# Row-wise logsumexp: VectorE sums each row as two halves in one pass, and the loads are cut anew

## The chip, the cores and the metric

The kernel runs on one core of a Trainium2 chip. Its time is the device time of one execution in microseconds (us); four runs of the kernel before gave a median of 163.52, from 163.41 to 163.89. Beside these times there is a profile of one execution. The engines that matter here are ScalarE (ACT), VectorE (DVE) and SyncE (SP), whose queue issues the loads, and the 16 DMA engines that carry them. GpSimd (POOL) only sets four constants and TensorE (PE) does nothing.

## The reference

The input is 32 x 512 rows of 1024 float32 values, 67.1 MB; the output is one number a row:

```python
def reference(x, axis):                      # x: (32, 512, 1024), axis = -1
    x_max = np.max(x, axis=axis, keepdims=True)
    return (x_max.squeeze(axis)
            + np.log(np.sum(np.exp(x - x_max), axis=axis))).astype(np.float32)
```

Both kernels leave the maximum out: they compute log(sum(exp(x))), which is the same number for values of this size, drawn from a normal distribution.

## The kernel before

**Tiling.** The 16384 rows are spread over 128 partitions, 128 rows for each partition. "A row" below means one row in every partition at once, so there are 128 of them, each 4 KB in a partition and 512 KB in all. They are loaded in 17 pieces, called load 0 to load 16; the list `CHUNKS` gives, for each load, its rows and how many of these are summed by DVE.

**The ring.** Loaded rows lie in `ring`, which has room for 51 rows. Loads take consecutive slots; a load that does not fit before the end of the ring begins again at slot 0. SP issues the loads in order (L84). Before a load into slots that were used, SP waits until the rows that lay there have been finished, by a count of finished instructions of DVE (`dve_done`) and one of ACT (`act_done`). Since the queue is in order, a load that waits holds back those behind it.

**The work on a load.** ACT waits until the load has landed. It takes the exponential of the first `n_dve` rows in one instruction, in place (L115), and DVE then sums them, all rows of the load in one reduction (L120):

```python
            nc.vector.wait_ge(act_done, acts)
            nc.vector.reduce_sum(
                out=sums[:, row : row + n_dve], in_=ring[:, s : s + n_dve], axis=AX
            ).then_inc(dve_done, 1)
```

Each other row of the load gets an ACT instruction of its own (L127), which takes the exponential and also gives the sum; in the trace this is a pair, ACTIVATE and ACTIVATION_READ_ACCUMULATOR. The sums of all rows gather in `sums`.

**The logarithms.** `take_logs` (L92) takes Ln of a stretch of `sums` into `res`. It is called twice: early, when ACT comes to load `LN_AT`, for the rows of all loads before it, and at the end for the rest. It runs on ACT and waits for the DVE and ACT work on its rows. At last ACT's queue stores `res`, 64 KB, to the output.

**Order.** The program is written out by hand; each engine runs its instructions in the order of the loop over `CHUNKS`, and no scheduler moves anything.

Of the kernel before, what the change touches and what calls it, by code (L numbers as in the profile page):

```python
# [1 line left out]

# [4 lines left out]

CHUNKS = [  # L10
    (4, 1), (15, 11), (16, 10), (16, 15), (16, 0), (14, 0), (12, 9), (9, 5), (7, 5), (5, 4),
    (4, 3), (3, 0), (2, 2), (2, 2), (1, 0), (1, 0), (1, 0),
]
RING_ROWS = 51

LN_AT = 5


@with_exitstack
def kernel(  # L20
    ctx: ExitStack,
    tc: tile.TileContext,
    x: bass.AP,
    axis: bass.AP,
    out: bass.AP,
):
    nc = tc.nc
    P = nc.NUM_PARTITIONS

    assert axis in (-1, len(x.shape) - 1), f"only last-axis reduction supported, got {axis}"  # L30

    x_flat = x.flatten_outer_dims()
    N, D = x_flat.shape
    assert N % P == 0
    NB = N // P
    assert sum(r for r, _ in CHUNKS) == NB

    fp32 = mybir.dt.float32
    Exp = mybir.ActivationFunctionType.Exp
    Ln = mybir.ActivationFunctionType.Ln  # L40
    AX = mybir.AxisListType.X

    x_v = x_flat.rearrange("(p t) d -> p t d", p=P)
    out_v = bass.AP(tensor=out.tensor, offset=out.offset, ap=[[NB, P], [1, NB]])

    ring = nc.alloc_sbuf_tensor("ring", [P, RING_ROWS, D], fp32).ap()
    sums = nc.alloc_sbuf_tensor("sums", [P, NB], fp32).ap()
    res = nc.alloc_sbuf_tensor("res", [P, NB], fp32).ap()

    landed = [nc.alloc_semaphore(f"landed{i}") for i in range(len(CHUNKS))]  # L50
    act_done = nc.alloc_semaphore("act_done")
    dve_done = nc.alloc_semaphore("dve_done")
    stored = nc.alloc_semaphore("stored")
    used = sorted(sem.num for sem in [*landed, act_done, dve_done])
    assert used == list(range(used[0], used[0] + len(used)))


    hook = nc.pop_inst_callback()
    symbolic, nc._always_lower_symbolic_ap = nc._always_lower_symbolic_ap, False


    place = []
    row = slot = 0
    for r, _ in CHUNKS:
        if slot + r > RING_ROWS:
            slot = 0
        place.append((slot, row))
        slot += r
        row += r

    busy = [(0, 0)] * RING_ROWS
    acts = dves = 0

    def load(i):
        (s, row), r = place[i], CHUNKS[i][0]
        act_wait = max(a for a, _ in busy[s : s + r])
        dve_wait = max(d for _, d in busy[s : s + r])
        if dve_wait:  # L80
            nc.sync.wait_ge(dve_done, dve_wait)
        if act_wait:
            nc.sync.wait_ge(act_done, act_wait)
        nc.sync.dma_start(out=ring[:, s : s + r], in_=x_v[:, row : row + r]).then_inc(  # L84
            landed[i], 16
        )

    def take_logs(lo, hi, dve_wait, act_wait):
        nonlocal acts
        nc.scalar.wait_ge(act_done, act_wait)  # L90
        nc.scalar.wait_ge(dve_done, dve_wait)
        nc.scalar.activation(out=res[:, lo:hi], in_=sums[:, lo:hi], func=Ln).then_inc(  # L92
            act_done, 1
        )
        acts += 1

    body = nc.main_func.blocks[-1]
    assert not body.instructions
    load(0)
    n_early = len(body.instructions)  # L100

    nc.scalar.preload_act_table_set("natural_log_exp_and_others")  # L102

    logged = 0
    done_before = [(0, 0)]
    for i, (r, n_dve) in enumerate(CHUNKS):
        if i:
            load(i)
        s, row = place[i]
        if i == LN_AT:  # L110
            logged = row
            take_logs(0, logged, *done_before[i])
        nc.scalar.wait_ge(landed[i], 16)
        if n_dve:
            nc.scalar.activation(  # L115
                out=ring[:, s : s + n_dve], in_=ring[:, s : s + n_dve], func=Exp
            ).then_inc(act_done, 1)
            acts += 1
            nc.vector.wait_ge(act_done, acts)
            nc.vector.reduce_sum(  # L120
                out=sums[:, row : row + n_dve], in_=ring[:, s : s + n_dve], axis=AX
            ).then_inc(dve_done, 1)
            dves += 1
            for j in range(n_dve):
                busy[s + j] = (0, dves)
        for j in range(n_dve, r):
            nc.scalar.activation(  # L127
                out=ring[:, s + j],
                in_=ring[:, s + j],
                func=Exp,  # L130
                accum_out=sums[:, row + j : row + j + 1],
            ).then_inc(act_done, 1)
            acts += 1
            busy[s + j] = (acts, 0)
        done_before.append((dves, acts))

    take_logs(logged, NB, dves, acts)
    nc.scalar.wait_ge(act_done, acts)
    nc.scalar.dma_start(out=out_v, in_=res).then_inc(stored, 16)


    nc.scalar.sem_clear(range(used[0], used[-1] + 1))


    first = nc.main_func.blocks[0]
    head, work = first.instructions, body.instructions
    end = next(k for k, i in enumerate(head) if i.opcode == "UnconditionalBranch")
    head, tail = head[:end], head[end:]
    for ins in work[:n_early]:
        at = next(  # L150
            k for k, i in enumerate(head) if i.engine == ins.engine and i.opcode == "Drain"
        )
        head.insert(at, ins)
    first.instructions = head + work[n_early:] + tail
    body.instructions = []

    nc._always_lower_symbolic_ap = symbolic
    nc.push_inst_callback(hook)


    tc.close()
    tc.compile()
    nc.gpsimd.wait_ge(stored, 16)
    nc.gpsimd.sem_inc(stored, -16)


# [1 line left out]
_INS = ['x', 'axis']  # L168
_OUTS = [((32, 512), 'float32')]

_NUMBERS = {'axis': -1}


# [26 lines left out]
```

The softmax here doesn't subtract the row's maximum and nothing guards it: scores larger than these inputs give would overflow.

## Time and profile before

| what | value |
|---|---|
| median of 4 runs | 163.52 us (163.41 to 163.89) |
| the profiled execution's own time | 163.41 us |
| its span, first to last instruction | 161.5 us |
| DVE busy | 72.9 us (45%), 11 reductions |
| ACT busy | 124.0 us (77%), 136 instructions |
| HBM read | 67.11 MB, 416 GB/s over the span |
| loads' queue | 96.9% of 16 DMA engines over the span |

All times of the trace count from the start of the span. A line of a group or of the time order names the line of the kernel, the engine, the operation, output and input, and how often it occurs; "idle before" is the time in which the engine had nothing to do just ahead of it, with what ended it. The profiled execution is 1.9 us longer than its span, which is start and end of the program outside the traced instructions. A recorded instruction can overlap the one behind it on its engine, so the distance between two starts is what an instruction costs in a full queue, and its recorded length is more.

### The profile page before, as it was taken

The numbers are of one execution on the slowest core, as the hardware profiler recorded it, in microseconds if no ns is written. First come the engines' busy times: TensorE is split into PE (matmuls) and PEld (weight loads), VectorE is DVE, ScalarE is ACT, GpSimd is POOL, SyncE is SP. The second block draws the span as 40 slices with busy tenths as digits, with TensorE's granted clock in tenths as the row PEclk, the third lists the DMA queues.
The fourth block names the chain that finished last, engine by engine and source line by source line (L and its number), as shares of the span: only waits on it lengthen the run. The fifth ranks groups of instructions, "written<-read, shape, count | busy, mean of one in ns | idle before, by whom it ended". The sixth has DMA issues, their size and how long they took to land.

```text
span 161.5 us, 212 instructions
## 1 busy us (share of the span) xinstructions
DVE 72.9 (45%) x11; ACT 124.0 (77%) x136; POOL 0.2 (0%) x4
## 2 busy tenths in 40 slices
DVE  0030000029960699000799920000004999799874
ACT  3190006997079990999419999999999999999995
POOL 0000000000000000000000000000000000000000
DMA  7999799989989989989979999999899999999990
GB/s 247 515 487 441 304 472 519 389 389 519 422 357 519 422 357 519 422 357 519 422 325 454 456 454 422 389 487 438 386 420 418 447 440 400 430 423 413 420 390 22
DMA packets 2593, 67.18 MB, mean 416 GB/s; under 512 B 288, under 2 KB 416, under 8 KB 800
## 3 DMA queue, kind: packets, MB, share of 16 engines
q1 hardware_dynamic: 2448, 67.11, 96.9%
q10 hardware_dynamic: 144, 0.07, 0.1%
q14 instruction: 1, 0.01, 0.0%
HBM read 67.11 MB, written 0.07 MB: 416 GB/s over the span
## 4 chain that ended last, share of the span: by engine, by line
ACT 52%; DMA 38%; DVE 7%; issue 1%
DMA ring<-in_x_dram 38%; ACT ring L127 30%; ACT ring L115 22%; DVE sums L120 7%; ACT res L92 0%
## 5 line engine op out<-in xcount | busy, mean ns | idle before, releaser
L120 DVE TENSOR_REDUCE sums<-ring 128x5 f32<-128x5120 f32 (+8 forms) x11 | 72.9, 6648 | 86.3 <-ACT ring L115 86.2
L115 ACT ACTIVATE ring<-ring 128x5120 f32<-128x5120 f32 (+8 forms) x11 | 59.3, 5394 | 29.7 <-DMA ring<-in_x_dram 29.7
L127 ACT ACTIVATE ring<-ring 128x1024 f32<-128x1024 f32 x61 | 63.4, 1040 | 5.3 <-DMA ring<-in_x_dram 5.3
L127 ACT ACTIVATION_READ_ACCUMULATOR ring<-ring 128x1 f32 x61 | 11.3, 186 | 0.0
L102 ACT ACT_TABLE_LOAD x1 | 1.3, 1283 | 0.8 <-PEq L181 0.8
L92 ACT ACTIVATE res<-sums 128x67 f32<-128x67 f32 (+1 forms) x2 | 0.5, 256 | 0.1
L181 POOL MEMSET const-bfloat16-1.0<- 128x1 bf16 x1 | 0.1, 102 | 0.0
L181 POOL MEMSET const-uint8-127<- 128x1 uint8 x1 | 0.1, 102 | 0.0
L181 POOL MEMSET const-float32-0.0<- 128x1 f32 x1 | 0.1, 99 | 0.2 <-issue 0.2
L181 POOL MEMSET const-float32-1.0<- 128x1 f32 x1 | 0.1, 99 | 0.0
## 6 DMA issues: line engine op xcount, KB each, us to landing
ring<-in_x_dram SPq DMA_DIRECT2D x1, 7680.0 KB, 24.9
ring<-in_x_dram SPq DMA_DIRECT2D x1, 7168.0 KB, 36.0
ring<-in_x_dram SPq DMA_DIRECT2D x1, 6144.0 KB, 21.6
ring<-in_x_dram SPq DMA_DIRECT2D x1, 4608.0 KB, 32.1
ring<-in_x_dram SPq DMA_DIRECT2D x2, 2048.0 KB, 26.4
ring<-in_x_dram SPq DMA_DIRECT2D x1, 3584.0 KB, 40.2
ring<-in_x_dram SPq DMA_DIRECT2D x1, 2560.0 KB, 44.4
ring<-in_x_dram SPq DMA_DIRECT2D x2, 1024.0 KB, 46.0
```

The costliest lines, as they stand in the source:

```text
L92: nc.scalar.activation(out=res[:, lo:hi], in_=sums[:, lo:hi], func=Ln).then_inc(act_done, 1)
L102: nc.scalar.preload_act_table_set("natural_log_exp_and_others")
L115: nc.scalar.activation(out=ring[:, s : s + n_dve], in_=ring[:, s : s + n_dve], func=Exp).then_inc(act_done, 1)
L120: nc.vector.reduce_sum(out=sums[:, row : row + n_dve], in_=ring[:, s : s + n_dve], axis=AX).then_inc(dve_done, 1)
L127: nc.scalar.activation(out=ring[:, s + j], in_=ring[:, s + j], func=Exp, accum_out=sums[:, row + j : row + j + 1],).then_inc(act_done, 1)
L181: nc = _bacc.Bacc("TRN2", target_bir_lowering=False, num_devices=1)
```

## The change

There are three edits.

- DVE's one reduction over the `n_dve` rows of a load becomes one instruction for each row. It reads the two halves of the row, 512 values each, as two inputs, adds them, writes the 512 sums over the first half in the ring, and adds them up into the row's place in `sums`. Built, each is two instructions, the main one on 128 x 512 and one that writes 128 x 1. Each counts `dve_done` up by one, so that a slot is known to be free row by row.
- `CHUNKS` has 16 loads in place of 17, with other sizes and other shares of DVE: 75 rows in all for DVE in place of 67, 53 for ACT alone in place of 61.
- The early Ln comes ahead of load 7 in place of load 5, and takes 96 columns in place of 67; the last Ln takes 32 in place of 61.

```diff
 CHUNKS = [
-    (4, 1), (15, 11), (16, 10), (16, 15), (16, 0), (14, 0), (12, 9), (9, 5), (7, 5), (5, 4),
-    (4, 3), (3, 0), (2, 2), (2, 2), (1, 0), (1, 0), (1, 0),
+    (4, 1), (16, 4), (16, 11), (16, 9), (16, 4), (16, 10), (12, 7), (9, 9), (7, 6), (5, 5),
+    (3, 3), (3, 3), (2, 2), (1, 0), (1, 1), (1, 0),
 ]
 RING_ROWS = 51
 
-LN_AT = 5
+LN_AT = 7
...
             nc.vector.wait_ge(act_done, acts)
-            nc.vector.reduce_sum(
-                out=sums[:, row : row + n_dve], in_=ring[:, s : s + n_dve], axis=AX
-            ).then_inc(dve_done, 1)
-            dves += 1
             for j in range(n_dve):
+                nc.vector.tensor_tensor_reduce(
+                    out=ring[:, s + j, : D // 2],
+                    in0=ring[:, s + j, : D // 2],
+                    in1=ring[:, s + j, D // 2 :],
+                    scale=1.0,
+                    scalar=0.0,
+                    op0=Add,
+                    op1=Add,
+                    accum_out=sums[:, row + j : row + j + 1],
+                ).then_inc(dve_done, 1)
+                dves += 1
                 busy[s + j] = (0, dves)
```

In the ring this puts loads 0 to 2 into slots 0 to 35 and load 3 into slots 0 to 15 again, load 4 into slots 16 to 31, load 5 into 32 to 47, load 6 into 0 to 11. Before, loads 0 to 3 filled slots 0 to 50, and load 4 took 0 to 15.

## The prediction

> **What bounds the kernel now.** I read the page first, its slices and queues, then stretches of time, then the instructions in order, then the chain that ended last.
>
> The page's slices of the span (DMA's share, in tenths, and GB/s) and its queue line:
>
> ```profile
> DMA  7999799989989989989979999999899999999990
> ...
> q1 hardware_dynamic: 2448, 67.11, 96.9%
> ```
>
> Busy time by stretch; columns are the stretch, its length, busy time of DVE, ACT and POOL, clock, DMA share and GB/s:
>
> ```profile
> 1.00:157.60 156.60, 71.32 (x11) 121.55 (x132) 0.00 (x0) 1.00 1.00 428
> 157.60:158.50 0.90, 0.90 (x1) 0.90 (x3) 0.00 (x0) 1.00 0.03 9
> 158.50:161.50 3.00, 0.65 (x1) 1.36 (x4) 0.00 (x0) 1.00 0.08 22
> ```
>
> From 1.0 to 157.6 us the 16 DMA engines never stop. The loads are the bound; ACT and DVE matter only where they are late after the last bytes, or where they free ring slots so late that the stream runs dry.
>
> The instructions in time order (start, length) show when loads landed, because ACT idles for each of the first five:
>
> ```profile
> 7.59 1.06 ACT L115 ACTIVATE ring<-ring 128x1024 f32<-128x1024 f32 x1 [5.54 <-DMA ring<-in_x_dram]
> 25.71 9.59 ACT L115 ACTIVATE ring<-ring 128x11264 f32<-128x11264 f32 x1 [13.94 <-DMA ring<-in_x_dram]
> 45.29 8.74 ACT L115 ACTIVATE ring<-ring 128x10240 f32<-128x10240 f32 x1 [5.84 <-DMA ring<-in_x_dram]
> 64.67 13.00 ACT L115 ACTIVATE ring<-ring 128x15360 f32<-128x15360 f32 x1 [4.41 <-DMA ring<-in_x_dram]
> 84.00 1.06 ACT L127 ACTIVATE ring<-ring 128x1024 f32<-128x1024 f32 x1 [5.29 <-DMA ring<-in_x_dram]
> ```
>
> A 16-row load lands 19.4 us after the one before it, 1.21 us a row. The last load was issued at 112.6 and took 45.7 us to land (the list of DMA issues), so it was there at 158.3 to 158.4. Loads 1 to 16 (109 rows after load 1, 15 loads) against the 16-row pitch give some 0.05 us for a load beside its rows.
>
> The end of the chain that ended last (start, length):
>
> ```profile
> 156.49 2.71 ACT ring L127 x5
> 159.20 0.22 issue
> 159.42 0.20 ACT ring L127
> 159.62 0.02 issue
> 159.64 0.25 ACT res L92
> ```
>
> ACT has had no idle time since 84.00; it starts the last row at 158.47, about 0.1 after that row landed, ends at 159.61, does the second Ln, and the store ends at 161.5.
>
> Durations by shape:
>
> ```profile
> L120 DVE TENSOR_REDUCE sums<-ring 128x15 f32<-128x15360 f32 x1 | 16.2, 16153 | 12.8 <-ACT ring L115 12.8
> L115 ACT ACTIVATE ring<-ring 128x9216 f32<-128x9216 f32 x1 | 7.9, 7872 | 0.0
> L120 DVE TENSOR_REDUCE sums<-ring 128x1 f32<-128x1024 f32 x1 | 1.2, 1220 | 8.7 <-ACT ring L115 8.7
> ```
>
> DVE: (16153 - 1220)/14336 = 1.0416 ns an element and 153 ns fixed. Queued back to back they overlap: in time order the 9-row and the 5-row reduction from 123.42 span 15.15, for 14 x 1.067 = 14.93 of elements and 0.15 fixed of the second, so the first pays about 70 ns. ACT likewise: a batch of n rows costs 0.853n + 0.096 us to the next start, a row with its own sum 1.0385 (853 + 93 + 93 for the accumulator read). The early Ln cost 0.325 (100.55 to 100.96 from the last read's start, less the usual 0.09).
>
> **What the Trainium skill says.** "VectorE: DVE Perf Modes", Two Vector instructions with no wait between them: an operation that writes out its accumulator is two instructions, and is not held where all operands start in the same quadrant, as here. The trace has no such DVE operation, but ACT's pairs agree. "Vector Engine (DVE) Microarchitecture Reference", 5.2 Measured stream behaviour: one- and two-source operations take 1.0417 ns an element (1.054 in a two-source program on contiguous data) and 75 ns an instruction; the trace has 1.0416 and 70 for one source. The same page, 7 Points that are easy to get wrong, says that scalar-tensor-tensor operations with two fp32 SBUF sources run at half rate. The trace can't settle that; it is a rival below.
>
> **The change, part by part.**
>
> *The row sum.* One DVE reduction over n rows, 1.067n + 0.07, becomes n pairs. Main: 512 x 1.0416 + 70 = 603 ns. Read: if it is paid like ACT's, as one more instruction, 71 ns. Sum d = 0.674 us a row. Bounds: 0.603 if the read hides; 0.691 with the skill's figures (540 + 75 + 76, an estimate); 0.84 if nothing overlaps (686 + 154); 1.21 at half rate (1066 + 70 + 71). I take 0.674. 75 rows make 50.5 us against 72.9; DVE is not the bound, so this alone buys nothing. What counts is how soon rows come free and the tail.
>
> *Load plan and ring.* Before, 4+15+16+16 = 51 rows fill the ring, so four loads go out unhindered. Now 4+16+16 = 36, a further 16 don't fit, and load 3 wraps to slot 0. New landings by 19.4 a load: 7.6, 27.0, 46.4, 65.8, 85.2, 104.6. Load 3 needs load 0 and 12 rows of load 1: ACT's batch of 4 (3.5) and 8 single rows (8.3) after 27.0, so issue at 38.9 for a stream that lasts to 46.4: hidden. Load 4 (slots 16 to 31) needs all 11 DVE rows of load 2. Batch Exp 46.4 + 9.6 = 56.0; 11d = 7.41; 0.08 for the end that the pitch doesn't count, 0.03 for the semaphore: issue at 63.5, with load 3 landing at 65.8. Before, load 4 was issued at 47.2 for 64.7. So 17 us of cover shrink to 2.3. How much lead does a load need? Load 0 gives the cold value: landed at 7.6 for 4 x 1.21 = 4.9 of data, 2.7. Below: data starts 1.0 after issue, and the last landing lies 0.5 or more after the last bytes moved, in every load, 1.5. I take 2.2: no gap, just. At 2.7 the gap is 0.4. I put 0.1 into the sum. SP's queue is in order: loads 5, 6, 7 stand behind load 4, but each needs rows that come free 19 us or more ahead of its data.
>
> *16 loads for 17*: -0.05 in the stream.
>
> *ACT's tail.* Before and after ACT is the last link. After load 5's landing (104.6): 46 batch rows x 0.853 = 39.25, 9 batches x 0.096 = 0.86, 14 single rows x 1.0385 = 14.54, the early Ln 0.325: 54.98, so the last read starts to be free at 159.60, and ends 0.09 later at 159.69. Before: 159.61. So +0.08, though the last load lands at 158.3.
>
> *DVE's tail.* Rows of loads 7 to 12 and 14 (29 of them) come after load 7's Exp at about 139.0. From load 9 on it runs from 149.6: 14d = 9.4, 159.0; the row of load 14 can't start before its Exp at 158.7, so 159.4. Hidden under ACT's 159.69 as long as 139.0 + 29d stays under it: d below 0.715.
>
> *Early Ln at load 7.* It waits for load 6's DVE rows: Exp done at 125.7, 7d = 4.7, 130.4; ACT gets there at 130.8. No wait up to d = 0.73. If it waited, load 7's Exp stands behind it, and all of DVE's tail behind that. Its price is the old Ln's, already counted; the last Ln takes 32 columns in place of 61, at 253 to 259 ns in either width.
>
> *Waits and counts.* The 64 more DVE increments (75 for 11) come at the ends of DVE's own instructions and no engine waits for them singly, but SP does gain: a row is released when it is summed, not with its batch, which is in the times above. DVE now also writes half of each row back into the ring; I put that at nothing, because DMA's rate did not differ between stretches with DVE busy and idle (the 16-row loads took 19.58, 19.38 and 19.33 us); if it costs, it shows as a longer d.
>
> Sum: span 161.5 + 0.08 + 0.1 = 161.7, with 1.9 around it (163.41 - 161.5) 163.6. The profiled execution lies 0.11 below the median of the runs, so in the median 163.7. A measurement of this kernel can tell about 0.2% (0.33 us) from no change; +0.2 us is 0.1%.
>
> **Rivals.** *Fifth load late, then DVE late* (d from 0.70 to 0.84): every 0.01 in d delays load 4 by 0.11 us and, past 0.715, DVE's end by 0.29 more. At d = 0.76: 11 x 0.086 = 0.95 of gap, and 139.0 + 0.95 + 22.0 = 162.0 for DVE against 160.6 for ACT: +2.3, 166.0. At d = 0.70: +0.15 to +0.6. For it: no row of the trace shows the fixed cost of a DVE operation with an accumulator. Against: one-source DVE instructions and ACT's pairs both overlap to the same 46 to 50% of their fixed time. It decides from d = 0.70 or so.
> *Half rate* (d = 1.21): load 4 is 5.7 late, Ln waits to 139.7, load 7's Exp ends at 147.8, and 29 x 1.21 = 35 more: 183, +23, 187. Against: the 1.054 ns measured on two 4-byte sources.
> *Faster*: the change frees DVE time, but a stream that is full for 156.6 us can shrink only by the 0.05 of a load, and ACT by its 0.1 of lateness: 163.3 at best, and only if ACT's tail is shorter than my sum.
> *The row sum brings nothing because DVE waits anyway*: that is my forecast; DVE's idle time before was 86 us, all for ACT.
>
> **How the numbers follow.** Forecast (d up to 0.70): 0.58, of which 0.50 within 0.2% and 0.08 above it (lead of 2.7 with d near 0.70, up to 164.2). Own range 163.4 to 164.2. Fifth load and DVE late: 0.29. Half rate: 0.08. Faster: 0.05. Faster by over 0.2% 0.05, within 0.50, slower 0.45. Range 163.3 to 165.6: the upper end is d = 0.75 with the lead at 2.2, and leaves out half rate and the worst of the second case.
>
> **What would show it.** A DVE pair pitch of 0.60 to 0.70; load 4 issued at 63.4 to 63.7 and landing at 85.2 to 85.6; DMA at full share around 65 us; no ACT idle after 104.6; no wait at the early Ln; ACT, not DVE, ahead of the last Ln. Wrong if the pair takes over 0.72, if the DMA share dips near 66 us by more than 0.5 us of stream, or if DVE releases the last Ln.

## The result

The changed kernel takes 163.70 us in the median (35 runs, 163.35 to 164.89) against 163.47 (55 runs, 163.12 to 163.96). The ratio is 1.0024, 95% interval 1.0015 to 1.0033; the medians differ by 0.23 us, 0.14%. The ratio is above that because 8 of the 35 single runs lie between 164.1 and 164.9, where none of the kernel before lies; the experiments come back to these. In the mean the difference is 0.39 us (163.87 to 163.48). So the time predicted, 163.7, is the median measured, and the sign is slower, at about the bound of 0.2% between no change and slower that the prediction had drawn.

The page of the changed kernel, the slices of the span and the loads' and the instructions' queues:

```profile
DMA  7996996997998997997998998899999999999990
...
q1 hardware_dynamic: 2304, 67.11, 96.7%
...
q14 instruction: 2, 0.02, 0.0%
```

The instructions' queue of the kernel before:

```profile
q14 instruction: 1, 0.01, 0.0%
```

DMA still sets the pace. The instructions' queue now carries two packets (0.02 MB) in place of one. The prediction has no term for this queue, and it turns out to matter.

Groups by line and shape: the operation, what it works on, count, then busy us and mean ns of one:

```profile
L121 DVE CUSTOM_DVE_ANT_0 ring<-ring 128x512 f32<-128x512 f32 x75 | 46.8, 687 | 112.6 <-ACT ring L115 112.6
L121 DVE DVE_READ_ACCUMULATOR2_ANT sums<- 128x1 f32 x75 | 6.2, 82 | 0.0
```

In time order (start, length):

```profile
55.99 0.69 DVE L121 CUSTOM_DVE_ANT_0 ring<-ring 128x512 f32<-128x512 f32 x1 [22.79 <-ACT ring L115]
56.61 0.08 DVE L121 DVE_READ_ACCUMULATOR2_ANT sums<- 128x1 f32 x1
56.61 0.68 DVE L121 CUSTOM_DVE_ANT_0 ring<-ring 128x512 f32<-128x512 f32 x1
57.22 0.08 DVE L121 DVE_READ_ACCUMULATOR2_ANT sums<- 128x1 f32 x1
57.22 0.68 DVE L121 CUSTOM_DVE_ANT_0 ring<-ring 128x512 f32<-128x512 f32 x1
```

A pair is 0.61 us from start to start. The read of the accumulator starts together with the next main instruction and adds next to nothing: 533 ns for 512 elements (at the 1.0416 of the prediction) and 78 fixed are the whole price of a row, and a one-source reduction alone had some 70 fixed. Half rate is out.

The landings of loads 3, 4 and 5, seen as the starts of ACT behind its idle time:

```profile
65.72 7.88 ACT L115 ACTIVATE ring<-ring 128x9216 f32<-128x9216 f32 x1 [4.56 <-DMA ring<-in_x_dram]
...
85.43 3.62 ACT L115 ACTIVATE ring<-ring 128x4096 f32<-128x4096 f32 x1 [4.55 <-DMA ring<-in_x_dram]
...
104.78 8.74 ACT L115 ACTIVATE ring<-ring 128x10240 f32<-128x10240 f32 x1 [3.27 <-DMA ring<-in_x_dram]
```

19.71 us from load 3 to load 4, where the others take 19.35. The chain that ended last shows what issued load 4, and when, and the end (start, length):

```profile
62.82 0.02 issue
62.84 0.33 SPq L84
63.17 0.05 issue
63.22 41.54 DMA ring<-in_x_dram
...
158.81 0.78 ACT ring L134
159.59 0.07 issue
159.66 0.20 ACT ring L134
159.85 0.02 issue
159.88 0.23 ACT res L92
```

Load 4 went out at 62.84, right behind the last DVE row of load 2. ACT's last read ends at 159.85, 0.24 after that of the kernel before; the span is 161.8 for 161.5.

### The profile page after: what moved, and what is told of

The parts are those of the page before. It is cut to its first block, busy times and chain, and to the rows that moved or that the text cites. A ratio compares the mean times of both kernels' runs of the same rounds, so it can differ in the third digit from the quotient of the medians.

```text
span 161.8 us, 338 instructions
## 1 busy us (share of the span) xinstructions
DVE 46.9 (29%) x150; ACT 122.8 (76%) x123; POOL 0.2 (0%) x4
## 4 chain that ended last, share of the span: by engine, by line
DMA 54%; ACT 40%; DVE 4%; issue 1%; SPq 0%
DMA ring<-in_x_dram 54%; ACT ring L115 31%; ACT ring L134 9%; DVE ring L121 4%; SPq L84 0%; ACT res L92 0%; DVE sums L121 0%
## 5 line engine op out<-in xcount | busy, mean ns | idle before, releaser
L115 ACT ACTIVATE ring<-ring 128x1024 f32<-128x1024 f32 (+9 forms) x14 | 66.3, 4765 | 36.5 <-DMA ring<-in_x_dram 36.5
L121 DVE CUSTOM_DVE_ANT_0 ring<-ring 128x512 f32<-128x512 f32 x75 | 46.8, 687 | 112.6 <-ACT ring L115 112.6
L134 ACT ACTIVATE ring<-ring 128x1024 f32<-128x1024 f32 x53 | 55.1, 1040 | 0.0
L134 ACT ACTIVATION_READ_ACCUMULATOR ring<-ring 128x1 f32 x53 | 9.9, 186 | 0.0
L121 DVE DVE_READ_ACCUMULATOR2_ANT sums<- 128x1 f32 x75 | 6.2, 82 | 0.0
L92 ACT ACTIVATE res<-sums 128x96 f32<-128x96 f32 (+1 forms) x2 | 0.5, 256 | 0.1
```

Source lines behind the costliest of these rows:

```text
L115: nc.scalar.activation(out=ring[:, s : s + n_dve], in_=ring[:, s : s + n_dve], func=Exp).then_inc(act_done, 1)
L121: nc.vector.tensor_tensor_reduce(out=ring[:, s + j, : D // 2], in0=ring[:, s + j, : D // 2], in1=ring[:, s + j, D // 2 :], scale=1.0, scal ...
L134: nc.scalar.activation(out=ring[:, s + j], in_=ring[:, s + j], func=Exp, accum_out=sums[:, row + j : row + j + 1],).then_inc(act_done, 1)
```

## The experiments

Four kernels were run first, to take the two suspects (load 4's late issue, ACT's tail) away one by one and together, and to run the operation alone. The kernel before had 163.49 in the median beside them. "Ratio" is to the kernel before, with its 95% interval in brackets.

**The slots of load 4 free earlier.**

```diff
-    (4, 1), (16, 4), (16, 11), (16, 9), ...
+    (4, 1), (16, 4), (16, 7), (16, 9), ...
```

> The changed kernel, but DVE takes 7 rows of load 2 in place of 11, and ACT 9 in place of 5, so that the slots of load 4 come free at about 57.8 us in place of 62.8. Theory (late load 4 costs the stream 0.2 to 0.35 us, though DMA never runs dry): load 4 lands 19.35 to 19.4 after load 3 in place of 19.71, load 5 at about 104.5, span 161.5 to 161.6, and the time falls by 0.15 to 0.3 us against the changed kernel, to about the kernel before. Rival (the 19.71 is scatter of the stream, and the difference is ACT's tail alone): load 4 may land at any of these, and the time stays within 0.1 us of the changed kernel, 0.2 to 0.4 over the kernel before.

Measured: 163.60 (21 runs), ratio to the kernel before 1.0010 [1.0003, 1.0017]. 0.10 less than the changed kernel in the median, and of the runs above 164.1 one in 21 is left, where the changed kernel had 8 in 35. The mean falls from 163.87 to 163.63. The gain in the median is below the theory's 0.15 to 0.3, at the edge of the rival's 0.1; the landing of load 4 behind load 3 was 19.33 (65.94 to 85.27), as the theory had it. But load 3, issued 7 us ahead, now came 19.8 behind load 2 (46.17 to 65.94), and the profiled span is 161.7. So a step of 0.3 to 0.4 in one load's landing also comes without a late issue. Something else makes it. The edit moved the two packets of the instructions' queue too: they begin at 69.6 and 79.3 in the changed kernel, both inside load 4, and at 50.1 (inside load 3) and 93.8 here.

**The early Ln ahead of load 5.**

```diff
-LN_AT = 7
+LN_AT = 5
```

> The changed kernel, but the early Ln comes ahead of load 5, where ACT waits 3.3 us for that load anyway, in place of load 7. Theory (ACT's chain after load 5 sets the end): the chain loses the 0.33 us of the Ln, and the end comes earlier by 0.2, until the last load itself sets it (158.5 landed, 0.02 to start, 1.13 for the last row: 159.64 in place of 159.85); span about 161.6. Rival (late load 4 sets the end by itself): no change from the changed kernel, span 161.8.

Measured: 163.68 (16 runs), 1.0023 [1.0009, 1.0037]: nothing gained, as the rival had it. 4 of its 16 runs are above 164.1, and its profiled execution is one of these (span 162.7). It shows what happened in this one. Time order, ACT at load 4:

```profile
86.38 3.62 ACT L115 ACTIVATE ring<-ring 128x4096 f32<-128x4096 f32 x1 [5.56 <-DMA ring<-in_x_dram]
```

Load 3 landed at 65.63 there, so load 4 took 20.7 us, 1.4 too many, with an issue at 62.8 as in the changed kernel. The trace has every DMA packet, and shows where that time goes. In this execution, in two stretches:

```profile
DMA packets 31, 0.98 MB, mean 1092 GB/s; under 512 B 16, under 2 KB 16, under 8 KB 16
...
DMA packets 1, 0.07 MB, mean 73 GB/s; under 512 B 0, under 2 KB 0, under 8 KB 0
```

The first is 64.4 to 65.3: 16 packets of 4 bytes end load 3, one for each DMA engine, and 15 engines begin their first packet of load 4. The second is 65.3 to 66.2: the 16th engine begins only at 66.13. It had nothing to do for over 1 us, and in this execution its part of load 4 lands 0.8 behind all others. Why this one engine and not the others, no run shows. In the changed kernel's own trace all 16 begin by 65.44, some of them after a wait of up to 0.3, and their first packets of load 4 take 2.42 to 2.67; with the early issue above all 16 take 2.42.

Where load 4 is issued at 57.6 to 57.7 (the kernel above and the one below) one run in 34 is above 164.1; where it is issued at 62.8, 12 in 51. That is the price of the short lead: mostly small, and 0.4 to 1.2 us over the median in a quarter of the executions. The packets of the instructions' queue are not the reason: they come at 69.7 and 79.3 here, after that engine's wait.

**Both.**

```diff
-    (4, 1), (16, 4), (16, 11), (16, 9), ...
+    (4, 1), (16, 4), (16, 7), (16, 9), ...
-LN_AT = 7
+LN_AT = 5
```

> Both of these edits: 7 DVE rows in load 2 and the early Ln ahead of load 5. Theory: they add, last row starts 0.02 to 0.1 after the last load has landed at about 158.2, ACT ends at 159.4 to 159.5, span 161.3 to 161.4, 0.1 to 0.2 us under the kernel before. If only one of the two causes is real: span 161.5 to 161.6, no better than that edit alone.

Measured: 163.60 (13 runs, none above 163.75), 1.0010 [1.0002, 1.0018]: the same as with the earlier load alone, which is what was expected if only one of the two causes is real. The end of the chain that ended last says why the Ln's place gives nothing:

```profile
117.82 34.25 DMA ring<-in_x_dram
152.07 0.02 issue
152.09 4.56 ACT ring L115 x2
156.66 1.04 ACT ring L134 x2
157.70 0.95 ACT ring L115
158.64 0.78 ACT ring L134
```

With the Ln out of the way ACT waits for load 11, which lands at 152.07, and from there the small loads alone give the end: batches of 3 and 2 rows, 1 row, 1, and the last take 7.6 us of ACT, while the last load lands 6.3 after load 11. So ACT's tail behind load 11 costs some 0.2 us here: 7.6 less 6.3 and the 1.1 that the last row takes in any case.

**The operation alone**, in the kernel before, with its 17 loads and its early Ln:

```diff
-            nc.vector.reduce_sum(
-                out=sums[:, row : row + n_dve], in_=ring[:, s : s + n_dve], axis=AX
-            ).then_inc(dve_done, 1)
+            for j in range(n_dve):
+                nc.vector.tensor_tensor_reduce(
...
```

> The kernel before with its own 17 loads, shares and early Ln at load 5, and only DVE's sum exchanged for the pass over two halves. Theory (the operation is off the path): DVE busy falls from 72.9 to about 42 us, everything else stays, span 161.4 to 161.6 and the time equal within 0.1 us. Rival (the operation itself costs: its writes into the ring slow the loads, or its program costs time outside the span): 0.2 us or more over the kernel before, with a longer stream or a longer difference between span and time.

Measured: 163.62 (21 runs), 1.0009 [1.0002, 1.0015], 0.13 over the kernel before, with DVE busy down to 42 us. That lies between the theory's bound of 0.1 and the rival's of 0.2; the difference between span and time is 1.9 as before. In the profiled execution load 4 lands 19.9 behind load 3 (64.36 to 84.26), though it was issued at 42.07, over 20 us ahead. Just before, from 82.8 to 83.2, the instructions' queue has a packet that the kernel before does not have:

```profile
q14 instruction: 1, 0.01, 4.8%
```

It is 8192 bytes, begins at 82.85 and takes 0.31 us of one DMA engine. The load's packet that begins right behind it, at 83.16, takes 2.69 where those beside it take 2.12. Load 4's part on one engine then lands 0.55 behind all others, and one engine trails, by 0.32 at the last load. New theory: 67 pairs are 134 DVE instructions where 11 stood, DVE's instructions have to be fetched once more while the program runs, and the fetch pushes back one of 16 engines that have no free time. The kernel waits for all 16 parts of a load, so a delay of the engine that ends last is the load's delay, and nothing later makes it up.

To test that, the fetches were had without the operation, and the operation without the fetch. Beside the next runs the kernel before had 163.48.

**More fetches without the operation.**

```diff
+EXTRA = {0: 192, 3: 320}
...
             dves += 1
+            for k in range(EXTRA.get(i, 0)):
+                nc.vector.memset(spare[:, i * 64 + k : i * 64 + k + 1], 0.0)
```

> The kernel before with 512 additional tiny DVE instructions (one value in each partition set to zero, in a place that nothing reads), 192 behind the sum of load 0 and 320 behind that of load 3, where DVE is idle for 25 and 30 us; their work is under 40 us in all. Theory (instruction fetches delay loads): four or five more 8 KB packets in the instruction queue, each putting 0.3 us on one of the 16 DMA engines, the last load later by 0.2 to 0.8 us, the time 0.2 to 0.8 over the kernel before. Rival (instruction fetches are hidden; the kernels with the new operation are slower for another reason): the time within 0.1 us of the kernel before.

Measured: 166.59 (4 runs), 1.0190 [1.0176, 1.0204], 3.1 us over the kernel before: the direction of the theory, four times the upper end of its range. The instruction queue, and busy time by stretch at the end (the last two columns are DMA share and GB/s):

```profile
q14 instruction: 5, 0.04, 0.1%
```

```profile
158.00:159.00 1.00, 1.00 (x1) 1.00 (x1) 0.00 (x0) 1.00 0.06 25
...
160.00:161.00 1.00, 1.00 (x2) 1.00 (x3) 0.00 (x0) 1.00 0.05 20
```

From 158 to 161 us the share is about 0.06: one engine of 16 still works, alone, at a sixteenth of the rate. The four additional fetches fell on the same engine: it trails by 1.4 after two of them and by 3.0 after four. A fetch puts it back by more than the 0.31 to 0.33 of the packet, since the load's packet right behind takes 0.55 to 0.66 longer than those beside it, as with the operation alone: 0.9 to 1.0 for each fetch in all. The engines of one load do not land together anyway (in the kernel before from 157.62 to 158.36 at the last load), so most of a first fetch can hide in that spread (0.13 us of it showed with the operation alone), and further ones on the same engine cannot. That fits four costing far more than four times one. DVE in time order shows the block that is fetched and the wait for it:

```profile
9.82 1.09 DVE L129 MEMSET spare<- 128x1 f32 x60
11.29 3.63 DVE L129 MEMSET spare<- 128x1 f32 x128 [0.38 <-issue]
17.49 0.15 DVE L129 MEMSET spare<- 128x1 f32 x4 [2.57 <-issue]
```

The instructions come in blocks of 128; a packet of 8192 bytes is then 64 bytes for each. The second stall, 2.57 us, ends behind the packet at 15.7. The Trainium skill, "Runtime: NRT & Kernel Launch", Instruction fetch mechanics, has blocks of 16 KiB and a cost that is mostly hidden; here the packets are of 8 KB, and with the DMA engines full the cost is not hidden.

**One fetch without the operation.**

```diff
+EXTRA = {3: 100}
...
+            for k in range(EXTRA.get(i, 0)):
+                nc.vector.memset(spare[:, k : k + 1], 0.0)
```

> The kernel before with 100 additional tiny DVE instructions (one value in each partition set to zero, in a place that nothing reads) behind the sum of load 3, where DVE is idle for 30 us: some 3 us of work that nobody waits for. That carries DVE past its 60th instruction, as the 75 pairs do, and calls for one more 8 KB fetch. Theory: one more packet in the instruction queue at about 95 to 105 us, one DMA engine trails by 0.3 to 1.0 more from there on, and the time rises by 0.1 to 0.4 us over the kernel before, as with the pairs alone (0.13). Rival (what costs 0.13 with the pairs is the operation, and the 3 us of the 512 instructions came from DVE's own stalls): within 0.05 of the kernel before.

Measured: 163.67 (14 runs), 1.0012 [1.0003, 1.0020], 0.19 over the kernel before. One packet of 8192 bytes more, at 99.8, and the last load lands at 158.53 for 158.36. Some 3 us of work in DVE's idle time, which carry it past its 60th instruction, cost as much as the 67 pairs, within the intervals. The same with fewer instructions, and so without the fetch, was not run; that it is the fetch rests on the packets.

**The operation without the fetch**, in the tail alone, where it also shortens ACT:

```diff
-    (4, 3), (3, 0), (2, 2), (2, 2), (1, 0), (1, 0), (1, 0),
+    (4, 4), (3, 3), (2, 2), (2, 2), (1, 1), (1, 1), (1, 0),
+PAIRS_FROM = 10
...
+            if i >= PAIRS_FROM:
+                for j in range(n_dve):
+                    nc.vector.tensor_tensor_reduce(
...
```

> The kernel before, where only the loads from the 11th on are changed: DVE takes 4, 3, 2, 2, 1, 1 of their rows in place of 3, 0, 2, 2, 0, 0, and sums these 13 rows by the pass over two halves; nothing else differs. Theory: 35 DVE instructions are too few for the additional 8 KB fetch of instructions that the fully changed kernels show (one packet at 50 to 94 us, after which one DMA engine trails by 0.3 to 0.6 us), so the trace has one such packet, ACT's at about 89, as before; ACT is 0.12 shorter in the tail and starts the last row within 0.05 of its landing; span 161.4, the time 0.05 to 0.15 us under the kernel before. Rival (the operation itself slows the loads, wherever it is used): no gain, or 0.1 over the kernel before.

> The kernel with the pass over two halves in the last loads alone, once more, for a narrower interval: 0.05 to 0.15 us under the kernel before, ratio 0.9990 to 0.9997. If its first result was chance, the ratio is 1.0 within 0.0003.

Measured: 163.36 (13 runs), 0.9993 [0.9985, 1.0001], and the second time 163.41 (22 runs), 0.9991 [0.9984, 0.9997]. The first alone could not tell it from no change; the second can, narrowly. It is faster than both kernels, by 0.07 to 0.12 us in the medians against the one before. ACT in time order at the end (second run):

```profile
154.66 3.80 ACT L117 ACTIVATE ring<-ring 128x2048 f32<-128x2048 f32 x3 [0.41 <-DMA ring<-in_x_dram]
158.45 1.06 ACT L144 ACTIVATE ring<-ring 128x1024 f32<-128x1024 f32 x1
159.41 0.19 ACT L144 ACTIVATION_READ_ACCUMULATOR ring<-ring 128x1 f32 x1
```

ACT has time to wait again, 0.41, and meets the last row as it lands. With 34 DVE instructions there is no fetch but ACT's own at 89 us, as before. That the operation itself, apart from its instructions, costs nothing is not shown further: here its effect and ACT's shorter tail come together, and their sum is what ACT's tail alone was expected to give.

**Load 4 later still.**

```diff
-    (4, 1), (16, 4), (16, 11), (16, 9), ...
+    (4, 1), (16, 4), (16, 13), (16, 9), ...
```

> The changed kernel, but DVE takes 13 rows of load 2 in place of 11, so that load 4 waits for 12 DVE rows behind a batch of 13: issue at 57.7 + 12 x 0.611 + 0.1 = 65.1 us in place of 62.8, 0.6 ahead of load 3's landing. Theory (a load needs some 3 us of lead, and part of it is lost from there on): load 4 lands 22.0 to 22.3 after load 3, all DMA engines pause by 1.5 us or more, span 163.9 to 164.4, the time 2.2 to 2.6 over the changed kernel. Rival of the prediction (a lead of 1.5 is enough): 0.9 over it.

Measured: 165.95 (4 runs), 1.0150 [1.0134, 1.0165], 2.25 over the changed kernel, as the theory had it. Busy time by stretch (a packet counts in the stretch in which it begins, so a share can be over 1):

```profile
64.00:66.00 2.00, 1.75 (x6) 0.28 (x1) 0.00 (x0) 1.00 0.00 0
66.00:68.00 2.00, 0.00 (x0) 2.00 (x1) 0.00 (x0) 1.00 1.57 524
```

No packet of data begins from 64 to 66; the first of load 4 begin at 66.13, and all 16 engines have stood idle. Load 4 was issued at 65.17 and landed at 87.80: 22.6, of which 19.4 are its data. So here a load needs 3.2 us of lead, and by the same sum 2.9 in the next kernel (67.82 to 90.09). In the changed kernel load 4 had 2.85.

**The new loads with the old sum.**

```diff
-                nc.vector.tensor_tensor_reduce(
...
+            nc.vector.reduce_sum(
+                out=sums[:, row : row + n_dve], in_=ring[:, s : s + n_dve], axis=AX
+            ).then_inc(dve_done, 1)
```

> The changed kernel with the 16 loads and the early Ln at load 7, but DVE's sum as in the kernel before: one reduction over the rows of a load. A row takes 1.07 us in place of 0.61 and all rows of a load come free together. Expected: load 4 issued at 56.0 + 11.8 = 67.9, 5 us after its issue in the changed kernel, the early Ln waits for load 6, and DVE ends last: 179 to 182 us. If the plan did not depend on the faster sum it would stay under 166.

Measured: 181.66, one run, within the expectation; load 4 went out at 67.82. The chain that ended last, near its end, is DVE:

```profile
146.37 21.61 DVE sums L120 x3
...
171.24 6.59 DVE sums L120 x3
```

The plan of loads lives on the short row: with 1.07 us a row it is 18 us slower, and with 0.61 no cost of it is seen but its short lead at load 4.

**The sum.** The operation alone is 0.13 over the kernel before. All of the change but the late load 4 is 0.11 over it, the same within the runs. All of it is 0.23. So about 0.12 is put down to the instruction fetch, about 0.12 in the median to the late load 4 (0.26 to 0.28 in the mean), and the 16 loads and the place of the Ln give nothing to be seen, or cancel. Each of these terms has an interval as wide as itself; what carries them is that the packets in the traces show both causes. The edit that issues load 4 earlier also moves the fetches from one load to another, so the 0.12 in the median may not be the late issue's alone; the late executions, which end with it, are the clearer sign.

## Why the prediction was right, and where it was not

- *The bound.* Right: the loads are the bound, and DVE's 112.6 us of idle time, all for ACT, show that its faster sum is worth nothing by itself.
- *Time of a row.* d = 0.674 was predicted, with 0.603 as the lower end if the read hides. It hides: 0.611. The step "if it is paid like ACT's, as one more instruction" failed; ACT's reads cost 93 ns each, DVE's add under 10.
- *Load 4.* Issue predicted at 63.5, measured 62.84, by that shorter row. The lead taken was 2.2, between 1.5 and 2.7; it is 2.9 to 3.2, so the upper end was too low, and the cold start of load 0 (2.7) was no bound for it. The two errors oppose each other, 0.7 against 0.7 to 1.0, and the 0.1 put into the sum came out near the 0.10 to 0.12 measured in the median. That is luck in part. In the mean of the runs the load costs more, 0.26 to 0.28, and the change 0.39 in place of the 0.2 of the sum. What the prediction had not thought of is the form of it: the stream does not run dry as a whole, but in some executions single engines do, and load 4 ends over 1 us late; in the one that was profiled, one engine began load 4 over 1 us late and landed 0.8 behind the others.
- *ACT's tail.* From load 5's landing to the end of the last read 54.98 + 0.09 = 55.07 were predicted; 104.78 to 159.85 is 55.07. But that this is what sets the end was only half right, and the 0.08 that it put into the sum is not found as a cost of its own: the early Ln, 0.33 of it, could be taken out with no gain, because ACT then waits for load 11, and the small loads behind it give nearly the same end. (Load 5's landing and the tail, 104.6 and 54.98, make 159.58, not 159.60; nothing hangs on it.)
- *DVE's tail and the early Ln.* No wait at the Ln, and the last row sum ends at 159.54, under ACT's 159.85, as worked out.
- *Waits and counts.* That the 64 more DVE increments hide holds for the increments. Not counted were the instructions themselves: 139 more for DVE, one more fetch, about 0.12 us. This term was missing from the sum, and it stands about where the 0.08 of ACT's tail stood: the 0.2 came out right in the median from other terms than those it was made of.
- *Rivals.* Fifth load late and then DVE late: the first half is there in its small form, the second not, since d is far under 0.70. Half rate: no. Faster: not with this change, but the 0.1 of ACT's lateness that it named is what the kernel with the pairs in the tail alone gets.

## What to carry to other kernels

Where the DMA engines have no free time, each block of instructions that has to be fetched holds up one of them, here by 0.8 to 1.0 us; the first showed as 0.1 to 0.2 us in the time, four more on one engine as 3.1. So count instructions, also on an engine that idles. A load that is to keep a stream unbroken had to be issued some 3 us before the stream's end here, and a short lead shows first in the scatter of the runs, less in the median. Use a faster operation where its latency is on the path (here 13 rows in the tail), and leave the long, single instruction where nothing waits for it.

## What the runs showed of the hardware that was not expected

- DVE's accumulator read after a two-input pass costs next to nothing in a full queue: pairs 0.611 us apart, 0.533 of it elements; ACT's costs 0.093.
- DVE fetches its instructions in blocks of 128 through the engines that carry the loads: the packet is 0.31 us, the load's packet behind it takes 0.5 to 0.7 longer, four more fetches on one engine left it 3.0 behind the others, and 163.48 became 166.59.
- An engine put back stays back: in the kernel with four more fetches it trailed by 3.0 at load 6, the first that ended after the last fetch, and by 3.0 at load 16.
- With a load issued 2.85 us before the one ahead of it landed, a quarter of the executions (12 of 51) took 0.4 to 1.2 us more than the median; in the one of these that was profiled, a single DMA engine of 16 stood idle for over 1 us.
